# A two-layer decoder trunk with its residual stream held tokens-first: w_out and w_down as 512-column strips past stationary tokens

## The chip, the core and the metric

One core of a Trainium2 chip runs the whole program. The metric is the device time of an execution in microseconds; before the change it is 2322.69 us, the median of three runs (2322.14 to 2322.91). Engines are named as in the profile: PE is TensorE with PEld its weight loads, DVE is VectorE, ACT is ScalarE, POOL is GpSimd, SP is SyncE, which issues the transfers.

## The reference

256 tokens of width 2048 pass through two layers, in float32:

```python
for l in range(DEPTH):
    h = rms_norm(x, attn_norm[l])
    proj = h @ w_in[l]                      # 2048 x 7184, split into heads' q, k, v and gates
    ...                                     # 4 heads of gated linear attention, 4 of retention
    mix = jnp.concatenate([o_gla, o_ret], axis=-1)
    x = x + mix @ w_out[l]                  # 2048 x 2048
    h = rms_norm(x, mlp_norm[l])
    x = x + jnp.square(jax.nn.relu(h @ w_up[l])) @ w_down[l]   # 2048 x 8192, 8192 x 2048
return rms_norm(x, final_norm)              # rms_norm: x * rsqrt(mean(x*x) + eps) * gain
```

## The kernel before

Every product is made of three. A float32 operand is split into a high part (rounded to fp32r by ACT) and a low part (the rest, by DVE), and high·high, high·low and low·high are added up in PSUM. Weights arrive from memory in pieces of 1 MB; each is split in two halves (`split`, one ACT cast `hi` and one DVE subtraction `lo` of 128x1024 each), of which `take` keeps two ahead of PE. The pools hold 3 raw pieces and 4 halves each of `hi` and `lo`, so a half is cast when PE has left the fourth half before it. Activations are tiles `z` of 128 x 512, the high part of 256 tokens beside the low one.

The residual stream `x` lies transposed: 128 features on the partitions, 16 k-tiles, 256 tokens along the free side. Two forms of matmul stand in the program:

- Weights stationary (`mm3`, `mat`; lines 239 and 241): for each k-tile the high weights meet all 512 columns of z and the low weights its 256 high ones. An output tile of 128 features takes 32 matmuls. w_up, w_down, w_out and half of w_in run so. The result of w_out and w_down is added to `x` by two DVE additions of 128x256 (`residual`).
- Tokens stationary (`wide`; lines 477 to 479): each half of the tokens of z is the stationary operand and a strip of up to 512 weight columns passes, three matmuls for each k-tile and token half. The rest of w_in runs so.

A layer is a chain of stages on PE: w_in with the heads between, w_out (16 tiles), then four blocks b, each 16 tiles of w_up (relu squared, split into z) and 16 of w_down. Sums of squares for a norm are made by ACT (`sq`) and DVE (`sqacc`), summed over partitions by matmuls with a column of ones (line 361, `Norm.scale`), made into reciprocal roots on POOL, and `spread` (line 372) turns these by a matmul into a tile R with a token in each column. A norm's gain is applied as x becomes z, R only behind the next product.

The order of the program is that of the code, with a scheduler that moves instructions a little by priority; each engine runs its own in order. `after(n, f)` puts a piece of work n `step()`s later, a step being a tile or a part of a strip.

Of the kernel before, what the change touches and what calls it, by code (L numbers as in the profile page):

```python
# [1 line left out]

# [7 lines left out]
F32 = mybir.dt.float32  # L10
# [6 lines left out]
P = 128  # L17
# [62 lines left out]
KEPT = 7  # L80
# [3 lines left out]
N_ATT, N_MLP, N_FIN, N_GLA, N_INV, N_N = 0, 32, 64, 80, 96, 97  # L84
# [31 lines left out]
def hybrid_kernel(ctx: ExitStack, tc: tile.TileContext, xT, positions, w_first, w_in_t, w_in_w, w_in_v0, w_in_n,  # L116
                  w_out_first, w_out, w_up, w_down, gate_up, norms, rows, consts, out):
# [16 lines left out]
    x = cp.tile([P, KT, S], F32, name="x")  # L134
# [45 lines left out]
    def w_pieces():  # L180
# [6 lines left out]
        for l in range(DEPTH):  # L187
# [67 lines left out]
    def mat_pair(zs):  # L255
# [9 lines left out]
        mm(0, w, range(8, 14))  # L265
        mm(1, take(), range(8))
        mm(0, w, range(14, 16))
# [59 lines left out]
    class Norm:  # L327


        def __init__(self, col):  # L330
            self.col, self.sums, self.z, self.R = col, [], [], None

# [7 lines left out]
        def square(self, k):  # L340
            sq = tmp("sq")
            A.activation(out=sq, in_=x[:, k, :], func=AF.Square)
            if k == 0 or k == KT - 1 and self.col is None:
                self.sums.append(sq)
            else:
                acc = tmp("sqacc")
                tt(acc, self.sums[0], sq, ALU.add)
                self.sums[0] = acc

        def add(self, k):  # L350
            if self.col is not None:
                self.scaled(k)
            self.square(k)

# [510 lines left out]
```

## Time and profile before

| | us |
|---|---|
| median of three runs | 2322.69 |
| the profiled execution | 2323.79 |
| its span, first to last instruction | 2322.0 |
| PE busy | 2297.7 |
| DVE busy | 1604.2 |
| ACT busy | 1059.2 |

PE's matmuls are pipelined: the duration of one holds its way through the array, and one starts before the one ahead of it has ended. Work on PE is therefore read from the distance between starts, or from how many fit into a window.

### The profile page before, as it was taken

What the parts mean: (1) busy time and instruction counts of PE and PEld (TensorE: products, weight loads), DVE (VectorE), ACT (ScalarE), POOL (GpSimd) and SP (SyncE); (2) the same over time, 40 slices, a digit from 0 to 9 for tenths busy, and PEclk for the clock granted to TensorE, in tenths of its full rate; (3) what the DMA queues carried; (4) which work ended last, traced back from release to release, by engine and by line L of the source; (5) the groups of instructions that cost most, each with busy time, mean ns of one, the idle gap of its engine ahead of it and who ended that gap; (6) DMA issues with size and microseconds to landing.
All of it is one profiled execution on the core that took longest, in us unless ns stands there. A gap on an engine that the chain in (4) does not pass through costs nothing.

```text
span 2322.0 us, 32691 instructions
## 1 busy us (share of the span) xinstructions
PE 2297.7 (99%) x13116; PEld 2002.4 (86%) x13116; DVE 1604.2 (69%) x2482; ACT 1059.2 (46%) x1467; POOL 90.6 (4%) x253
## 2 busy tenths in 40 slices
PE   8999999999999999999999999999999999999997
PEld 7888888888888888888898888988888888888886
DVE  7777777676576576577767777776766766766765
ACT  5444544544344344345544444454434434434442
POOL 3001001000000000000000101000000000000000
PEclk9999999999999999999999999999999999999999
DMA  7544545555555555555554445455555555555553
GB/s 258 178 169 177 193 170 183 192 187 184 192 187 189 192 184 197 182 192 189 185 181 179 173 175 178 162 187 184 194 185 189 192 184 196 182 194 187 186 195 109
DMA packets 61034, 429.13 MB, mean 185 GB/s; under 512 B 6849, under 2 KB 7105, under 8 KB 10450
## 3 DMA queue, kind: packets, MB, share of 16 engines
q1 hardware_dynamic: 60738, 427.00, 53.1%
q8 instruction: 102, 1.67, 0.3%
q14 instruction: 50, 0.41, 0.0%
q10 hardware_dynamic: 144, 0.05, 0.0%
HBM read 424.92 MB, written 2.10 MB: 184 GB/s over the span
## 4 chain that ended last, share of the span: by engine, by line
PE 97%; DVE 1%; POOL 1%; issue 0%; DMA 0%; ACT 0%; DVEq 0%; POOLq 0%
PE acc L239 53%; PE acc L241 26%; PE acc L477 5%; PE acc L478 5%; PE acc L479 5%; POOL rs_t L155 1%; PE ps_s L594 0%; PE ps_v L479 0%; PE ps_v L478 0%; PE ps_v L477 0%; PE ps_t L695 0%; PE ps_s L623 0%; DVE z L158 0%; PE ps_o L643 0%; PE ps_o L644 0%
## 5 line engine op out<-in xcount | busy, mean ns | idle before, releaser
L239 PE MATMUL acc<-z,hi 128*128 128x512 f32 x5376 | 1692.8, 396 | 6.7 <-ACT hi L212 6.7
L212 ACT CAST hi<-raw 128x1024 fp32r<-128x1024 f32 (+1 forms) x808 | 840.2, 1042 | 1157.1 <-PE acc L239 752.8
L155 DVE TENSOR_TENSOR lo<-raw,hi 128x1024 fp32r<-128x1024 f32 (+1 forms) x808 | 979.1, 1215 | 516.3 <-ACT hi L212 514.2
L241 PEld LDWEIGHTS acc<-z,lo 128*128 128x128 f32 x5376 | 1011.0, 188 | 242.8 <-DVE lo L155 4.0
L241 PE MATMUL acc<-z,lo 128*128 128x256 f32 x5376 | 1057.9, 278 | 2.4 <-DVE lo L155 2.4
L239 PEld LDWEIGHTS acc<-z,hi 128*128 128x128 f32 x5376 | 820.4, 189 | 9.0 <-ACT hi L212 6.7
L155 DVE TENSOR_TENSOR x<-x,acc 128x256 f32<-128x256 f32 x320 | 133.8, 420 | 126.6 <-PE acc L241 121.7
L477 PE MATMUL acc<-hi,z 128*128 128x512 f32 (+2 forms) x576 | 206.6, 360 | 0.0
L478 PE MATMUL acc<-lo,z 128*128 128x512 f32 (+2 forms) x576 | 204.8, 356 | 0.0
L479 PE MATMUL acc<-hi,z 128*128 128x512 f32 (+2 forms) x576 | 204.6, 355 | 0.0
L479 PEld LDWEIGHTS acc<-hi,z 128*128 128x128 f32 x576 | 109.2, 190 | 15.3
L477 PEld LDWEIGHTS acc<-hi,z 128*128 128x128 f32 x576 | 109.2, 190 | 15.1
L478 PEld LDWEIGHTS acc<-lo,z 128*128 128x128 f32 x576 | 109.3, 190 | 14.3
L155 DVE TENSOR_TENSOR sum<-acc,right 128x256 f32<-128x256 f32 x176 | 73.2, 416 | 3.2 <-ACT right L292 3.2
L292 ACT COPY right<-acc 128x256 f32<-128x256 f32 x176 | 64.4, 366 | 2.2 <-PE acc L241 2.2
L158 DVE SCALAR_TENSOR_TENSOR uu<-ug 128x256 f32<-128x256 f32 x128 | 54.3, 424 | 4.4
L155 DVE TENSOR_TENSOR ug<-sum,R 128x256 f32<-128x256 f32 x128 | 54.4, 425 | 4.2
L540 DVE RECIPROCAL ge<-ge 128x256 f32<-128x256 f32 x32 | 54.6, 1732 | 0.2
L155 DVE TENSOR_TENSOR z<-uu,z 128x256 fp32r<-128x256 f32 x128 | 53.4, 418 | 0.0
L303 ACT CAST z<-uu 128x256 fp32r<-128x256 f32 x128 | 51.5, 404 | 0.1
L155 POOL TENSOR_TENSOR rs_t<-rs_y 128x2 f32<-128x2 f32 x48 | 20.5, 427 | 593.2 <-DVE rs_y L315 590.7
L155 POOL TENSOR_TENSOR rs_t<-r_tok 128x2 f32<-128x2 f32 x12 | 8.8, 731 | 887.1 <-DVE r_tok L315 886.5
(130 smaller groups left out, 757.5 us busy)
## 6 DMA issues: line engine op xcount, KB each, us to landing
raw<-w_up SPq DMA_DIRECT2D x128, 1024.0 KB, 4.9
raw<-w_down SPq DMA_DIRECT2D x128, 1024.0 KB, 4.9
raw<-w_in_w SPq DMA_DIRECT2D x48, 1024.0 KB, 4.8
raw<-w_in_t SPq DMA_DIRECT2D x44, 1024.0 KB, 4.7
raw<-w_out SPq DMA_DIRECT2D x24, 1024.0 KB, 5.0
raw<-w_in_n SPq DMA_DIRECT2D x12, 1024.0 KB, 5.0
raw<-w_out_first SPq DMA_DIRECT2D x8, 1024.0 KB, 5.2
raw<-w_in_v SPq DMA_DIRECT2D x8, 544.0 KB, 4.0
```

Of the source, the lines that this page charges most:

```text
L155: return (e or V).tensor_tensor(out=out, in0=a, in1=b, op=op)
L158: return V.scalar_tensor_tensor(out=out, in0=a, scalar=s, in1=b, op0=op0, op1=op1)
L212: A.copy(out=hi[:, :n], in_=raw)
L239: T.matmul(acc, hi[:, ws[i]], zs[i], start=(k + i == 0), stop=False)
L241: T.matmul(acc[:, :S], lo[:, ws[i]], zs[i][:, :S], start=False, stop=(k + i == KT - 1))
L292: A.copy(out=r, in_=acc[:, S:])
L303: A.copy(out=z[:, :S], in_=src)
L477: T.matmul(ps[t][:, :n], zh, hi[:, ks], start=(k == 0), stop=False)
L478: T.matmul(ps[t][:, :n], zh, lo[:, ks], start=False, stop=False)
L479: T.matmul(ps[t][:, :n], zl, hi[:, ks], start=False, stop=(k == KT - 1))
L540: V.reciprocal(out=e, in_=e)
```

## The change

- x's residual is kept as `xt`, tokens on the partitions, 2 x 2048 numbers each. It's loaded as a second copy of x (`x_tok`, 2 MB) into the place of the transposed x when the first norm has used that.
- w_out and each block of w_down run as four strips of 512 columns past stationary tokens (`strip`), their weights laid out for it in memory. A strip ends in one DVE addition of 128x512 for each half of the tokens.
- Sums of squares come from ACT alone: `Square` over 512 columns with a sum along the row (`TokenNorm.square`), for each strip and token half; DVE adds the four. The matmuls with ones go, but for the first norm.
- For each norm that a product follows, PE transposes `xt` back (`TokenNorm.transpose`): 8 transposes of 128x128 for a strip of 512 features, two steps behind the strip, and those of the last strip between the halves of the first tile of the next product (`mat_pair` with `between`). ACT and DVE make z from the transposes' PSUM. `spread` follows those two tiles.
- The end: the gain is multiplied in as a row (`fin`), the last strip keeps its last four pieces and runs them for one token half and then the other (`kept=4`), and each half is scaled and stored on its own (`finish`), with no matmul.

```diff
-            for i in range(KT // 4):
-                yield w_out_first[l, i], 2
-            for m in range(NFIRST, KT):
-                yield w_out[l, m - NFIRST], 2
+            for c in range(NC):
+                for u in range(4):
+                    yield w_out[l, c, u], 2
             for b in range(NFB):
                 for f in range(FB):
                     yield w_up[l, b * FB + f], 2
-                for m in range(KT):
-                    yield w_down[l, b, m], 2
+                for c in range(NC):
+                    for u in range(4):
+                        yield w_down[l, b, c, u], 2
...
-    def mat_pair(zs):
+    def mat_pair(zs, between):
 
         accs = [new_acc(), new_acc()]
 
@@ -262,29 +264,50 @@
 
         mm(0, take(), range(8))
         w = take()
-        mm(0, w, range(8, 14))
+        between()
+        mm(0, w, range(8, 12))
         mm(1, take(), range(8))
-        mm(0, w, range(14, 16))
+        mm(0, w, range(12, 16))
         mm(1, take(), range(8, 16))
         return accs
 
-    def mats(zs, order, before, done):
+    def strip(zs, order, done, kept=1, every=2):
+
+        ps = [new_acc() for t in range(NT)]
+        left = []
+
+        def mm(u, t, hi, lo):
+            for kk in range(2):
+                z, ks = zs[order[2 * u + kk]], slice(kk * SW, (kk + 1) * SW)
+                zh, zl = z[:, t * P:(t + 1) * P], z[:, S + t * P:S + (t + 1) * P]
+                T.matmul(ps[t], zh, hi[:, ks], start=(u + kk == 0), stop=False)
+                T.matmul(ps[t], zh, lo[:, ks], start=False, stop=False)
+                T.matmul(ps[t], zl, hi[:, ks], start=False, stop=(2 * u + kk == KT - 1))
+
+        for u in range(KT // 2):
+            w = take(AHEAD if u < KT // 2 - kept else min(AHEAD, kept - 1))
+            if u < KT // 2 - kept:
+                for t in range(NT):
+                    mm(u, t, *w)
+                if u % every == every - 1:
+                    step()
+            else:
+                left.append((u, *w))
+        for t in range(NT):
+            for u, hi, lo in left:
+                mm(u, t, hi, lo)
+            done(t, ps[t])
+
+    def mats(zs, before, done):
 
         accs = [new_acc() for _ in range(NFIRST)]
-        kept = []
         for i in range(KT // 2):
             before(i)
             hi, lo = take(min(i, AHEAD))
-            if i < KEPT:
-                for m in range(NFIRST):
-                    mm3(accs[m], hi, lo, (m, NFIRST + m), [zs[order[2 * i + kk]] for kk in range(2)], 2 * i)
-            else:
-                kept.append((hi, lo))
-        for m in range(NFIRST):
-            for i, (hi, lo) in enumerate(kept):
-                k = 2 * (KEPT + i)
-                mm3(accs[m], hi, lo, (m, NFIRST + m), [zs[order[k + kk]] for kk in range(2)], k)
-            done(m, accs[m])
+            for m in range(NFIRST):
+                mm3(accs[m], hi, lo, (m, NFIRST + m), zs[2 * i:2 * i + 2], 2 * i)
+                if i == KT // 2 - 1:
+                    done(m, accs[m])
 
...
-        def square(self, k):
-            sq = tmp("sq")
-            A.activation(out=sq, in_=x[:, k, :], func=AF.Square)
-            if k == 0 or k == KT - 1 and self.col is None:
-                self.sums.append(sq)
-            else:
-                acc = tmp("sqacc")
-                tt(acc, self.sums[0], sq, ALU.add)
-                self.sums[0] = acc
-
-        def add(self, k):
-            if self.col is not None:
-                self.scaled(k)
-            self.square(k)
...
+    class TokenNorm(Norm):
+
+
+        def __init__(self, col):
+            self.col, self.z, self.R = col, [None] * KT, None
+            self.sq = sp.tile([P, NT, NC], F32, tag="sq", name="sq", bufs=2)
+            self.r = cp.tile([P, NT], F32, tag="r_tok", name="r_tok", bufs=2)
+
+        def square(self, c, t, ps):
+            A.activation(out=ps, in_=xt[:, t, c * SW:(c + 1) * SW], func=AF.Square,
+                         accum_out=self.sq[:, t, c:c + 1])
+
+        def transpose(self, c):
+            for k in range(c * SW // P, (c + 1) * SW // P, 2):
+                pt = mxp.tile([P, 2, S], F32, tag="mx", name="ps_x")
+                for i in range(2):
+                    for t in range(NT):
+                        T.transpose(pt[:, i, t * P:(t + 1) * P], xt[:, t, (k + i) * P:(k + i + 1) * P], ident)
+                for i in range(2):
+                    f = self.col + k + i
+                    self.z[k + i] = to_z(pt[:, i, :], nrm[:, f:f + 1])
+
+        def scale(self, e=G, ts=slice(0, NT)):
+            n = ts.stop - ts.start
+            v = sp.tile([P, NT], F32, tag="rv", name="rv")
+            V.tensor_reduce(out=v[:, :n], in_=self.sq[:, ts, :], axis=mybir.AxisListType.X, op=ALU.add)
+            V.tensor_scalar(out=v[:, :n], in0=v[:, :n], scalar1=1.0 / D, scalar2=EPS, op0=ALU.mult, op1=ALU.add)
+            rsqrt(v[:, :n], n, self.r[:, ts], e)
 
     pending, now = [], [0]
 
...
+    def finish(norm, t):
+
+        norm.scale(V, slice(t, t + 1))
+        for i, (a, b) in enumerate(((0, 512), (512, 1024), (1024, 1536), (1536, 2048))):
+            xc = xt[:, t, a:b]
+            if i % 2:
+                A.activation(out=xc, in_=xc, func=AF.Copy, scale=norm.r[:, t:t + 1])
+            else:
+                V.tensor_scalar(out=xc, in0=xc, scalar1=norm.r[:, t:t + 1], scalar2=None, op0=ALU.mult)
+            nc.sync.dma_start(out=out[:, t, a:b], in_=xc)
+
+    mats(norm.z, begin, lambda m, acc: first.append(total(acc)))
     rotary_tables()
 
...
+        def begin_norm():
+            norm.transpose(NC - 1)
+            norm.scale()
+
         plan = w_in_plan()
+        if l:
+            first = [total(a) for a in mat_pair(z_att, begin_norm)]
         for n, (what, g, part, h, _) in enumerate(plan):
             if what == "w":
                 wide(g, n == len(plan) - 1)
             else:
                 d = st.setdefault((g, h), {})
-                a = first[n] if l == 0 and n < NFIRST else total(mat(z_att))
+                a = first[n] if n < len(first) else total(mat(z_att))
                 if part == "k0" and g == "g":
...
@@ -725,30 +776,31 @@
                         first_head = l == 0 and h == 0
                         after(SC + 3 * first_head, ret_scores, h)
                         after(OU + 2 * first_head, head_out, g, h)
-            n0 = NFIRST - 1 if l == 0 else 0
-            if n == n0:
-                norm.scale()
-                after(3 if l == 0 else 2, spread)
+            if n == len(first) - 1:
+                if l == 0:
+                    norm.scale()
+                after(3 if l == 0 else 1, spread)
+            if l == 0 and n == NFIRST + 2:
+                xt = cp.tile([P, NT, D], F32, tag="x", name="xt")
+                nc.sync.dma_start(out=xt, in_=x_tok)
             step()
 
-        def residual(acc, m):
-            tt(x[:, m, :], x[:, m, :], acc[:, :S], ALU.add)
-            tt(x[:, m, :], x[:, m, :], acc[:, S:], ALU.add)
-
-        norm = Norm(N_MLP + l * KT)
-
-        def out_tile(m, acc):
-            residual(acc, m)
-            norm.add(m)
-
-        mats(mix, MIX_ORDER, lambda i: i and step(), out_tile)
-        for m in range(NFIRST, KT):
-            out_tile(m, mat(mix))
+        def add(norm, c, t, ps, fin=None):
+            xc = xt[:, t, c * SW:(c + 1) * SW]
+            tt(xc, xc, ps, ALU.add)
+            if norm is not None:
+                norm.square(c, t, ps)
+                if fin is not None:
+                    tt(xc, xc, fin[:, c * SW:(c + 1) * SW], ALU.mult)
+                elif t == NT - 1 and c < NC - 1:
+                    after(2, norm.transpose, c)
+
+        norm = TokenNorm(N_MLP + l * KT)
+        for c in range(NC):
+            strip(mix, MIX_ORDER, partial(add, norm, c), every=1 if c == 0 else 2)
             step()
 
-        after(1, norm.scale)
-        after(2, norm.spread)
-        nxt = Norm(N_ATT + (l + 1) * KT if l + 1 < DEPTH else None)
+        nxt, fin = None, None
         late = []
 
         def up(a, us, f):
@@ -765,31 +817,29 @@
 
         for b in range(NFB):
             us = [None] * FB
+            if b == 0:
+                two = mat_pair(norm.z, begin_norm)
+                after(1, norm.spread)
             for f in range(FB):
-                a = total(mat(norm.z))
+                a = total(two[f] if b == 0 and f < 2 else mat(norm.z))
                 step()
                 up(a, us, f)
-            accs = mat_pair(us)
-            for m in range(KT):
-                acc = accs[m] if m < 2 else mat(us)
-                residual(acc, m)
-                if b == NFB - 1:
-                    nxt.add(m)
-                    if l + 1 == DEPTH:
-                        V.tensor_scalar(out=x[:, m, :], in0=x[:, m, :], scalar1=nrm[:, N_FIN + m:N_FIN + m + 1],
-                                        scalar2=None, op0=ALU.mult)
+            if b == NFB - 1:
+                nxt = TokenNorm(N_ATT + (l + 1) * KT if l + 1 < DEPTH else None)
+                if l + 1 == DEPTH:
+                    fin = cp.tile([P, D], F32, tag="row", name="fin")
+                    nc.sync.dma_start(out=fin, in_=gain.broadcast_to([P, D]))
+            for c in range(NC):
+                last = fin is not None and c == NC - 1
+
+                def done(t, ps):
+                    add(nxt, c, t, ps, fin)
+                    if last:
+                        finish(nxt, t)
+
+                strip(us, range(KT), done, 4 if last else 1)
                 step()
         norm = nxt
-
-    norm.scale(V)
-    norm.spread(False)
-    R = norm.R.rearrange("p (k s) -> p k s", k=1)
-    k = 0
-    for n in (1, 3, 4, 4, 4):
-        xs = x[:, k:k + n, :]
-        tt(xs, xs, R.broadcast_to([P, n, S]), ALU.mult)
-        nc.sync.dma_start(out=out[:, k:k + n, :], in_=xs)
-        k += n
```

The order on PE within a block of w_down, one output tile and its k-tiles. Before (`z_` are activations, `hi_` and `lo_` one half-piece of weights, `acc_` a bank of PSUM):

```order
L239 MATMUL acc_5873<-z_4736,hi_5831 128x512
L239 MATMUL acc_5873<-z_4790,hi_5831 128x512
L241 MATMUL acc_5873<-z_4736,lo_5832 128x256
L241 MATMUL acc_5873<-z_4790,lo_5832 128x256
L239 MATMUL acc_5873<-z_4844,hi_5831 128x512
L239 MATMUL acc_5873<-z_4898,hi_5831 128x512
```

and now, one piece of a strip (the two banks are the two halves of the tokens):

```order
L283 MATMUL acc_5296<-hi_5388,z_5103 128x512
L284 MATMUL acc_5296<-lo_5389,z_5103 128x512
L285 MATMUL acc_5296<-hi_5388,z_5103 128x512
L283 MATMUL acc_5296<-hi_5388,z_5157 128x512
L284 MATMUL acc_5296<-lo_5389,z_5157 128x512
L285 MATMUL acc_5296<-hi_5388,z_5157 128x512
L283 MATMUL acc_5297<-hi_5388,z_5103 128x512
L284 MATMUL acc_5297<-lo_5389,z_5103 128x512
```

Every matmul now has 512 moving columns, which are weights; a pair of k-tiles takes 12 of them for 512 output columns, where it took 16 of mixed width.

The order on DVE where the first layer's w_out ends and w_up begins. Before (`x_` is the transposed residual, `z_4436` the last k-tile of the MLP's input, `sum` and later rows belong to w_up):

```order
L155 TENSOR_TENSOR lo_4447<-raw_4444,hi_4446 128x1024
L155 TENSOR_TENSOR x_88<-x_88,acc_4391 128x256 x2
L155 TENSOR_TENSOR lo_4467<-raw_4444,hi_4466 128x1024
L158 SCALAR_TENSOR_TENSOR z_4436<-x_88,nrm_90,z_4436 128x256
L155 TENSOR_TENSOR sqacc_4441<-sqacc_4389,sq_4439 128x256
L155 TENSOR_TENSOR lo_4515<-raw_4512,hi_4514 128x1024
L363 TENSOR_SCALAR rv_4493<-ps_r_4490 128x2
```

and now (`acc_4083` and `acc_4084` are the token halves of the last strip, `lo_4256` and `lo_4276` the two halves of w_up's second tile, `ps_x` the transposes):

```order
L157 TENSOR_TENSOR lo_4256<-raw_4253,hi_4255 128x1024
L157 TENSOR_TENSOR xt_787<-xt_787,acc_4083 128x512
L157 TENSOR_TENSOR xt_787<-xt_787,acc_4084 128x512
L157 TENSOR_TENSOR lo_4276<-raw_4253,hi_4275 128x1024
L411 TENSOR_REDUCE rv_4301<-sq_3545 128x2
...
L157 TENSOR_TENSOR lo_4330<-raw_4327,hi_4329 128x1024
L160 SCALAR_TENSOR_TENSOR z_4284<-ps_x_4279,nrm_90,z_4284 128x256
```

The last four z of the next product stand behind the two additions, a reduction and two casts of later weights; before, the last z stood behind two additions and one cast. On PE the same place reads, before:

```order
L239 MATMUL acc<-z,hi 128x512 x2
L241 MATMUL acc<-z,lo 128x256 x2
L361 MATMUL ps_r<-cst,sqacc 128x1 x2
L239 MATMUL acc<-z,hi 128x512 x2
L241 MATMUL acc<-z,lo 128x256 x2
```

and now, from the strip's last matmuls to the second half of w_up's first tile:

```order
L284 MATMUL acc<-lo,z 128x512
L285 MATMUL acc<-hi,z 128x512
L241 MATMUL acc<-z,hi 128x512 x2
L243 MATMUL acc<-z,lo 128x256 x2
...
L243 MATMUL acc<-z,lo 128x256 x2
L403 MATMUL ps_x<-cst,xt 128x128 x8
L241 MATMUL acc<-z,hi 128x512 x2
```

Between the strip and the eight transposes stand 16 matmuls, the first eight k-tiles of one tile of w_up.

## Rows read from the trace of the kernel before

**Rows 1.** The page: PE's busy time, and the chain that ended last, by engine.
```profile
PE 2297.7 (99%) x13116; PEld 2002.4 (86%) x13116; DVE 1604.2 (69%) x2482; ACT 1059.2 (46%) x1467; POOL 90.6 (4%) x253
...
PE 97%; DVE 1%; POOL 1%; issue 0%; DMA 0%; ACT 0%; DVEq 0%; POOLq 0%
```

**Rows 2.** Windows (from:to, length; busy and count by engine; PEclk, DMA share, GB/s).
```profile
549.00:638.00 89.00, 89.00 (x513) 77.68 (x512) 53.29 (x67) 34.17 (x34) 0.00 (x0) 1.00 0.58 195
```

**Rows 3.** Timeline of PE (start, length, count) in a tile of w_down.
```profile
599.96 0.63 PE L239 MATMUL acc<-z,hi 128*128 128x512 f32 x2
600.42 0.39 PE L241 MATMUL acc<-z,lo 128*128 128x256 f32 x2
600.65 0.63 PE L239 MATMUL acc<-z,hi 128*128 128x512 f32 x2
```

**Rows 4.** Timeline of PE, a w_in strip: its first matmul, and what follows its 48th.
```profile
138.36 0.40 PE L477 MATMUL acc<-hi,z 128*128 128x512 f32 x1
...
149.28 0.60 PE L695 MATMUL ps_t<-cst,on 128*128 128x128 f32 x4
```

**Rows 5.** Timeline of PE, a head's four transposes and what follows them.
```profile
371.38 0.60 PE L695 MATMUL ps_t<-cst,on 128*128 128x128 f32 x4
371.74 0.72 PE L239 MATMUL acc<-z,hi 128*128 128x512 f32 x2
372.30 0.40 PE L241 MATMUL acc<-z,lo 128*128 128x256 f32 x2
```

**Rows 6.** Timeline of PE behind w_out: the sums of squares, and spread.
```profile
452.88 0.50 PE L361 MATMUL ps_r<-cst,sqacc 128*128 128x1 f32 x4
453.24 0.70 PE L239 MATMUL acc<-z,hi 128*128 128x512 f32 x2
...
459.36 0.71 PE L372 MATMUL ps_R<-cst,r_tok 128*128 128x128 f32 x4 [0.30 <-POOL r_tok L155]
```

**Rows 7.** Lines (names, shapes, count | busy us, mean ns of one | idle before).
```profile
L155 DVE TENSOR_TENSOR lo<-raw,hi 128x1024 fp32r<-128x1024 f32 (+1 forms) x808 | 979.1, 1215 | 516.3 <-ACT hi L212 514.2
...
L212 ACT CAST hi<-raw 128x1024 fp32r<-128x1024 f32 (+1 forms) x808 | 840.2, 1042 | 1157.1 <-PE acc L239 752.8 <-issue 209.8 <-PE acc L479 135.3
...
L155 DVE TENSOR_TENSOR x<-x,acc 128x256 f32<-128x256 f32 x320 | 133.8, 420 | 126.6 <-PE acc L241 121.7
...
L306 ACT ACTIVATE z<-ps_t,nrm 128x256 fp32r<-128x256 f32 x16 | 7.6, 474 | 14.3 <-DVE z L158 14.3
...
L427 ACT ACTIVATE z<-x 128x512 f32<-128x512 f32 x8 | 4.9, 616 | 0.0
```

**Rows 8.** Timeline of the end of the program.
```profile
2306.99 0.39 PE L241 MATMUL acc<-z,lo 128*128 128x256 f32 x2
2307.42 0.88 DVE L155 TENSOR_TENSOR x<-x,acc 128x256 f32<-128x256 f32 x2 [3.52 <-PE acc L241]
...
2309.66 0.16 DVE L363 TENSOR_SCALAR rv<-ps_r 128x2 f32<-128x2 f32 x1 [0.53 <-PE ps_r L361]
...
2311.82 0.16 DVE L158 SCALAR_TENSOR_TENSOR r_tok<-rs_t,r_tok 128x2 f32<-128x2 f32 x1
...
2313.30 4.68 DVE L155 TENSOR_TENSOR x<-x,ps_R 128x256 f32<-128x256 f32 x5 [1.31 <-PE ps_R L372]
```

**Rows 9.** DMA issues of the output (count, KB each, median us to landing).
```profile
y<-x SPq DMA_DIRECT2D x3, 512.0 KB, 2.9
...
y<-x SPq DMA_DIRECT2D x1, 384.0 KB, 2.4
```

**Rows 10.** Timeline of SP in the first w_in: three loads of one strip.
```profile
24.64 7.66 SPq L223 DMA_DIRECT2D raw<-w_in_v  x3
```

**Rows 11.** Timeline of PE: the first use of the w_in_n pieces.
```profile
50.37 0.59 PE L477 MATMUL acc<-hi,z 128*128 128x256 f32 x2
```

**Rows 12.** Timeline of PE: the spread of the first norm.
```profile
41.76 1.06 PE L372 MATMUL ps_R<-cst,r_tok 128*128 128x128 f32 x4 [1.81 <-POOL r_tok L155]
```

**Rows 13.** Window of PE behind that spread (columns as rows 2, PE alone).
```profile
42.50:45.20 2.70, 2.70 (x14) 0.50 0.19 79
```

More of the change, by code (lines that the diff above doesn't have):

```diff
@@ L1 @@
 from contextlib import ExitStack
+from functools import partial
 import numpy as np
@@ L79 @@
 AHEAD = 2
-KEPT = 7
+NC = 4
+SW = D // NC
 X_CUTS = {0: (2, 4), 1: (4, 6), 2: (6, 10), 4: (10, 16)}
@@ L116, in hybrid_kernel @@
 def hybrid_kernel(ctx: ExitStack, tc: tile.TileContext, xT, positions, w_first, w_in_t, w_in_w, w_in_v0, w_in_n,
-                  w_out_first, w_out, w_up, w_down, gate_up, norms, rows, consts, out):
+                  w_out, w_up, w_down, gate_up, norms, rows, gain, x_tok, consts, out):
     nc = tc.nc
@@ L132, in hybrid_kernel @@
     V, A, G, T = nc.vector, nc.scalar, nc.gpsimd, nc.tensor
-    x = cp.tile([P, KT, S], F32, name="x")
+    x = cp.tile([P, KT, S], F32, tag="x", name="x")
     cst = cp.tile([P, C_N], F32, name="cst")
@@ L330, in __init__ @@
         def __init__(self, col):
-            self.col, self.sums, self.z, self.R = col, [], [], None
+            self.col, self.z, self.R = col, [], None
         def scaled(self, k):
@@ L366, in scale, with spread @@
             self.r = r
-        def spread(self, keep=True):
+        def spread(self):
             ps = mxp.tile([P, 512], F32, tag="mx", name="ps_R")
@@ L373, in spread @@
                          start=True, stop=True)
-            if keep:
-                R = cp.tile([P, S], F32, tag="R", name="R", bufs=2)
-                A.copy(out=R, in_=ps[:, :S])
-                self.R = R
-            else:
-                self.R = ps[:, :S]
+            R = cp.tile([P, S], F32, tag="R", name="R", bufs=2)
+            A.copy(out=R, in_=ps[:, :S])
+            self.R = R
+    class TokenNorm(Norm):
[21 more added lines that the diff above has]
+            rsqrt(v[:, :n], n, self.r[:, ts], e)
     pending, now = [], [0]
@@ L406, in load_x @@
         nc.sync.dma_start(out=x[:, a:b, :], in_=xT[:, a:b, :])
-    norm = Norm(N_ATT)
+    norm, xt = Norm(N_ATT), None
     sqs = ztile().bitcast(F32)
-    norm.sums = [sqs]
+    norm.sums = sqs
     first = []
@@ L431, in begin @@
             rotary_angles()
-    mats(norm.z, range(KT), begin, lambda m, acc: first.append(total(acc)))
+    def finish(norm, t):
[8 more added lines that the diff above has]
+    mats(norm.z, begin, lambda m, acc: first.append(total(acc)))
     rotary_tables()
@@ L833 @@
     wides = [np.concatenate([w_in[:, :, p[3]:p[3] + p[4]] for p in parts], axis=2) for parts, _ in wide_plan()]
-    w_out_first = a["w_out"].reshape(DEPTH, KT, P, D)[:, MIX_ORDER, :, :NFIRST * P]
+    chunks = lambda w: np.stack(np.split(w, NC, axis=-1), axis=-3)
+    w_out = a["w_out"].reshape(DEPTH, KT, P, D)[:, MIX_ORDER].reshape(DEPTH, D, D)
     w_down = a["w_down"].reshape(DEPTH, NFB, FB * P, D)
+    x = a["x"][0]
     arrays = {
-        "xT": np.ascontiguousarray(a["x"][0].reshape(S, KT, P).transpose(2, 1, 0)),
+        "xT": np.ascontiguousarray(x.reshape(S, KT, P).transpose(2, 1, 0)),
         "positions": np.ascontiguousarray(a["positions"]),
@@ L843 @@
         "w_in_n": strips_of(np.stack([w for w in wides if w.shape[2] == DV], axis=1), 2),
-        "w_out_first": first_of(w_out_first.reshape(DEPTH, D, NFIRST * P), 4),
-        "w_out": tiles_of(a["w_out"][:, :, NFIRST * P:]),
+        "w_out": strips_of(chunks(w_out), 4),
         "w_up": tiles_of(a["w_up"]),
-        "w_down": tiles_of(w_down),
+        "w_down": strips_of(chunks(w_down), 4),
         "gate_up": np.ascontiguousarray(
@@ L850 @@
         "norms": np.ascontiguousarray(np.concatenate(
-            [columns(a[n]) for n in ("attn_norm", "mlp_norm", "final_norm", "gla_out_norm")]
+            [columns(a[n]) for n in ("attn_norm", "mlp_norm", "gla_out_norm")]
             + [(10000.0 ** (-np.arange(0, DV, 2) / DV)).astype(np.float32)[:, None]], axis=1)),
         "rows": np.ascontiguousarray(np.concatenate([a["ret_norm_gain"], a["ret_norm_bias"]], axis=1)),
+        "gain": a["final_norm"][None],
+        "x_tok": np.ascontiguousarray(x.reshape(NT, P, D).transpose(1, 0, 2)),
         "consts": constants(),
@@ L858 @@
             for n, v in arrays.items()]
-    args.append(nc.dram_tensor("y", (P, KT, S), F32, kind="ExternalOutput").ap())
+    args.append(nc.dram_tensor("y", (P, NT, D), F32, kind="ExternalOutput").ap())
     with tile.TileContext(nc) as tc:
@@ L863 @@
     y = r.results[0]["y"]
-    return np.ascontiguousarray(y.transpose(2, 1, 0)).reshape(1, S, D)
+    return np.ascontiguousarray(y.transpose(1, 0, 2)).reshape(1, S, D)
```

4 lines of the change are left out of this document (2 added, 2 removed).

## The prediction

> **What bounds the kernel now.** I read the busy time of each engine first, then the chain of waits, then TensorE (PE) in order of time in four places. PE is busy for 2297.7 of 2322.0 us, and the chain that ended last is 97% PE [rows 1]. So a change counts by what it does to the spacing of matmuls on PE, and at the two ends of the program, where PE isn't fed. The stretches by window say that a stage of 16 tiles is stall-free: some 512 matmuls in 89.0 us at granted clock 1.00, the 2.4 GHz level, with VectorE busy for 53.3 us and ScalarE for 34.2 [rows 2]. The timeline of one such tile shows the beat: two matmuls of 256 columns take 0.23 us together [rows 3], and of the mean beat of four, 89.0 / 128 = 0.695 us, 0.465 are left for the two of 512 columns. That is 116 and 232.5 ns a matmul, start to start; the durations printed in those rows overlap and are no spacing.
>
> The strips that the change brings to w_out and w_down have a model in the kernel of before: the 512-column strips of w_in, where tokens are stationary. There 48 matmuls of 512 columns run from 138.36 to 149.28 us, 227.5 ns each [rows 4].
>
> **Term 1, the strips.** A stage (w_out, or one block of w_down) multiplies 16 k-tiles by 16 column tiles. Before: 256 matmuls of 512 columns and 256 of 256, 196,608 columns, 89.0 us [rows 2]. After: 16 k-tiles x 4 strips x 2 token halves x 3 products = 384 matmuls of 512 columns, the same 196,608 columns in 128 instructions fewer. At 227.5 ns that is 87.4 us, 1.6 us less. There are 2 x (1 + 4) = 10 such stages: -16.4 us. No row shows such a strip in these stages, so the bounds are the two spacings of a 512-column matmul in this trace: 227.5 ns [rows 4] gives -16.4, 232.5 ns [rows 2, 3] gives 10 x (384 x 0.2325 - 89.0) = +2.8. I take the lower, since that row is the same instruction sequence (zh·hi, zh·lo, zl·hi, all 512 wide) and 232.5 belongs to a 512 that alternates with 256s. A gain beyond -16.4 would need a spacing that no row has; I allow 1 ns either side, some 4 us.
>
> **Term 2, the transposes.** Three norms (both MLP norms and the second layer's first) now get their input by 32 transposes each, in 12 groups of 8. Four transposes of a head take from 371.38 to 371.74, and the pair of 512s behind them 0.56 us instead of 0.465 [rows 5]. Eight: twice 0.36 plus some 0.07, since only the last of a group overlaps its successor, plus 0.09, so 0.88 us. 12 x 0.88 = +10.6 us, bounds 9.7 (twice 0.36 + 0.09) and 11.6 (0.97 with the pairs wholly apart).
>
> **Term 3, the sums of squares by matmul.** For those three norms the group of four L361 goes: 452.88 to 453.24 [rows 6], and the same 0.09 us behind it, 0.45 us. -1.3 us.
>
> **Term 4, the wait of spread.** PE sits 0.30 us for POOL's r_tok before the spread, which stands one tile (5.6 us) behind the sums [rows 6]. Now the spread stands behind two tiles and the sums need no PE. 3 x 0.3 = -0.9 us, between 0 and -0.9.
>
> **Term 5, the end.** Before: the last matmuls end at about 2307.22 (2306.99 plus 0.23), the add starts at 2307.42, the reciprocal root runs from 2309.66 to 2311.98, then come the spread and five products with their stores; the products end at 2317.98, and 4.0 us for the last issue, its landing (2.9 us of 512 KB) and the closing follow, to 2322.0 [rows 3, 8, 9]. That is 14.8 us behind the last matmul. After: token half 0 is finished beneath the last 24 matmuls of half 1 (24 x 0.2275 = 5.5 us). For half 1: 0.2 to start; an add of 128x512, 0.70 (between 0.42 for 256 and 1.215 for 1024 elements); a square of 128x512, 0.62; gaps 0.1; reduction 0.2 and the same root 2.3; two scalings on ScalarE 1.3; the same 4.0 less 0.7, since a 256 KB store should land in 2.2 us (384 KB took 2.4); 0.5 for the queue of four issues [rows 7 to 9]. Sum 9.2 us. -5.6 us; with add and square at either neighbour's price (0.42 to 1.2 each) -6.1 to -4.5.
>
> **What costs nothing, and its cover.** At each of the three hand-overs the last transposes need the add of the second token half. Let T be the end of a strip. The order rows put one low-part cast and both adds on VectorE ahead. That cast needs the buffer which PE frees at T - 2.7 (12 matmuls earlier): rounding 1.04, cast 1.2, so it ends near T - 0.3; adds end near T + 0.4 and T + 1.1 [rows 7]. PE runs 16 matmuls, four beats of 0.70 us, first: the transposes start at T + 2.8. Cover 1.7 us. Their z are wanted at T + 2.8 + 0.9 + 4.2 = T + 7.9 at the earliest; behind one more rounding, four scalings of 0.47 and their low parts are done at about T + 7.2, and the last two of them are wanted at T + 8.6. The residual adds fall from 32 x 0.42 to 8 x 0.70 us a stage on VectorE, off the path. At the other strip borders three pieces are cast ahead of the adds and the fourth, behind them, is wanted 8.2 us after T (36 matmuls of the next strip), so no price. If the cover goes, see rival C.
>
> The token copy of x (2.1 MB) is issued on SP when the third of a strip's w_in_v loads is out, at 32.30, ahead of the two w_in_n loads, whose strip starts at 50.37 [rows 10, 11]. At the 195 GB/s of rows 2 the copy lasts until 43.1, one w_in_n load behind it until 48.5; rounding and low part (1.04 + 1.2) end at 50.7, the high part at 49.5. Cost 0 to 0.5 us; I take 0. The 1 MB for the final gain goes out where layer 1 has its row load.
>
> **Sum.** -16.4 + 10.6 - 1.3 - 0.9 - 5.6 = -13.6 us. The profiled execution took 2323.8 (its span 2322.0 and 1.8 around it): 2310.2 after. The median of the runs shown, 2322.69, is 1.1 below it: 2309.1, so 2309 us.
>
> **Rivals.** A: matmuls cost by column, not by instruction. Then 196,608 columns cost 89.0 us whatever their cut, term 1 is 0 and the sum +2.8: 2325.5 us, which is no change. For it: the columns make most of a stage, and a quarter fewer instructions change the spacing by under 2% in the rows there are. Against it: 1536 columns take 695 ns in four matmuls [rows 2] and 3 x 227.5 = 682.5 ns in three [rows 4], so the fourth instruction costs 12.5 ns.
> The Trainium skill, "TensorE: Matmul & The Clock Gate", section "Back-to-back issue gap", puts that fixed part at about 2.5 ns: by it the 128 instructions are worth 0.32 us a stage, term 1 an estimated -3.2 us, and the sum about zero. The trace doesn't agree (12.5 ns), so A gets little.
>
> B, the slower one: in w_out and w_down a 512-column matmul keeps the 232.5 ns that it has there now, because these stages carry more transfers and casts (DMA share 0.58 [rows 2]) than the w_in strip of rows 4. Place: all 10 stages; price +2.8 instead of -16.4, so +5.6 in all: 2328.3 us, and 3.8 us more for each further ns. It decides from 10 x (384 s - 89.0) + 2.8 > 4.6, a spacing s above 232.2 ns. Against it: rows 3 mix two widths, rows 4 don't, and both run beside casts of the same kind of pieces.
>
> C: the cover at the hand-overs fails (casts late, VectorE's queue in another order). PE then waits as ahead of 41.76, 1.8 us, behind which the granted clock was 0.50, the 1.2 GHz level, for 2.7 us [rows 12, 13], of which half is lost: 3.2 us at each of three places, +9.5: 2318.6 us.
>
> **Chances.** Forecast 0.78, A 0.09, B 0.07, C 0.06. About 0.2%, 4.6 us, is what a measurement here can tell from no change. Forecast and half of C are faster (0.80, a hundredth taken off for a forecast that runs short), A, the rest of C and that hundredth are no change (0.12), B and a hundredth of A are slower (0.08). Forecast with its own bounds (strip spacing 1 ns either way 4, transposes 1, end 1, small waits up to 5 more): 2303 to 2317; with C to 2320. A and B lie outside.
>
> **What would show it.** PE's matmul records fall from 13116 by 1280 + 20 + 4 and rise by 96, to about 11,908. A w_down stage takes 87.4 us with matmuls 227 ns apart; 232 or more says B, 89.0 A. Each group of eight transposes delays PE by 0.9 us. No idle PE longer than 0.3 us from 50 us on, and clock 1.00 throughout; a wait on VectorE before the transposes, or on a z in the second tile behind a strip, says C. The span ends 9 to 10 us behind the last matmul. The forecast is wrong if the spacing of the strips isn't that of rows 4.

## The result, and the profile after

The changed kernel takes 2308.44 us (median of 4 runs, 2307.11 to 2309.43), beside 2322.44 for the kernel before in 4 runs: ratio 0.9939, 95% interval [0.9922, 0.9956]. A second set of runs gave 2308.25 against 2323.14, 0.9936 [0.9924, 0.9949]. The forecast was 2309.0. The profiled execution took 2307.11 us with a span of 2305.3, 16.7 us shorter than the span of before; the medians are 14.0 apart, so one profiled execution of each flatters the change by about 2.7 us.

The page after, in answer to [rows 1]:

```profile
PE 2281.8 (99%) x11908; PEld 1949.2 (85%) x11908; DVE 1507.1 (65%) x2191; ACT 1057.6 (46%) x1471; POOL 88.1 (4%) x253
...
PE 98%; DVE 1%; DMA 0%; issue 0%; ACT 0%; POOL 0%; ACTq 0%; DVEq 0%
```

PE is still the bound, with the 11,908 matmuls that were forecast. Next, windows cut exactly from a stage's first matmul to the next stage's first (from:to, length, busy and count by engine, granted clock, DMA share, GB/s): of before one block of w_down,

```profile
716.30:805.47 89.17, 89.17 (x514) 77.80 (x513) 52.62 (x66) 34.10 (x35) 0.00 (x0) 1.00 0.56 190
```

and of after the same block of w_down, a block of w_up, and the first w_up behind a norm:

```profile
716.08:803.13 87.05, 87.05 (x386) 72.08 (x385) 44.51 (x43) 34.30 (x34) 0.00 (x0) 1.00 0.55 192
626.92:716.08 89.16, 89.16 (x513) 77.80 (x512) 62.99 (x94) 42.27 (x62) 0.00 (x0) 1.00 0.54 191
449.38:539.87 90.49, 90.49 (x526) 79.14 (x524) 65.25 (x102) 45.58 (x71) 3.36 (x12) 1.00 0.54 188
```

A block of w_down falls by 2.12 us, at the same clock of 1.00 (the 2.4 GHz level) and with PE busy throughout in both. A block of w_up, whose code is the same, stays at 89.17 (before, 627.13 to 716.30) and 89.16. w_out, which holds three groups of transposes as well, goes from 91.60 to 92.09.

The hand-over from w_out to w_up in the timeline of after, where a strip ends at T = 449.38 (start, length, engine, operation, count, idle before):

```profile
449.09 1.28 DVE L157 TENSOR_TENSOR xt<-xt,acc 128x512 f32<-128x512 f32 x2
...
449.15 0.39 PE L285 MATMUL acc<-hi,z 128*128 128x512 f32 x1
449.38 0.62 PE L241 MATMUL acc<-z,hi 128*128 128x512 f32 x2
...
451.93 0.39 PE L243 MATMUL acc<-z,lo 128*128 128x256 f32 x2
452.16 1.04 PE L403 MATMUL ps_x<-cst,xt 128*128 128x128 f32 x8
452.95 0.70 PE L241 MATMUL acc<-z,hi 128*128 128x512 f32 x2
...
461.16 0.40 PE L243 MATMUL acc<-z,lo 128*128 128x256 f32 x2
461.39 0.61 PE L380 MATMUL ps_R<-cst,r_tok 128*128 128x128 f32 x4
461.75 0.71 PE L241 MATMUL acc<-z,hi 128*128 128x512 f32 x2
```

Both additions are done at 450.37, the transposes start at 452.16, and eight of them hold the next matmul up to 452.95. The spread waits for nothing, where it waited 0.30 us before [rows 6]. Around that spread, the timeline of before has

```profile
458.66 0.40 PE L241 MATMUL acc<-z,lo 128*128 128x256 f32 x2
...
459.83 0.71 PE L239 MATMUL acc<-z,hi 128*128 128x512 f32 x2
```

so that the way from the 256s ahead of it to the 512s behind it falls from 1.17 us to 0.59.

The end of after, in answer to [rows 8]:

```profile
2294.66 0.39 PE L285 MATMUL acc<-hi,z 128*128 128x512 f32 x1
2295.09 0.69 DVE L157 TENSOR_TENSOR xt<-xt,acc 128x512 f32<-128x512 f32 x1
2295.81 0.60 ACT L395 ACTIVATE acc<-xt 128x512 f32<-128x512 f32 x1 [0.23 <-DVE xt L157]
2296.34 0.19 ACT L395 ACTIVATION_READ_ACCUMULATOR acc<-xt 128x1 f32 x1
2296.56 0.69 DVE L157 TENSOR_TENSOR xt<-xt,fin 128x512 f32<-128x512 f32 x1 [0.79 <-ACT acc L395]
2297.17 0.15 DVE L411 TENSOR_REDUCE rv<-sq 128x1 f32<-128x4 f32 x1
...
2299.66 1.33 ACT L473 ACTIVATE xt<-xt,r_tok 128x512 f32<-128x512 f32 x2 [3.13 <-DVE r_tok L160]
```

The last matmul starts at 2294.66 and the span ends at 2305.3.

One thing got worse. PE's waits up to 75 us (engine, tile and line, what it waited for, us in total, times, longest) are, before,

```profile
PE acc L239 <- ACT hi L212: 6.7, 1, 6.7
PE acc L241 <- DVE lo L155: 2.4, 2, 2.2
PE ps_R L372 <- POOL r_tok L155: 1.8, 1, 1.8
```

and after:

```profile
PE acc L241 <- ACT hi L214: 7.2, 1, 7.2
PE acc L243 <- DVE lo L157: 3.0, 2, 2.3
PE ps_R L380 <- POOL r_tok L157: 1.8, 1, 1.8
PE ps_gr L552 <- ACT gr L535: 0.5, 1, 0.5
PE ps_o L687 <- DMA raw<-w_in_t: 0.5, 1, 0.5
PE acc L523 <- DVE lo L157: 0.2, 1, 0.2
```

The last three are new. They sit between 49 and 56 us. ScalarE's timeline there shows why; before:

```profile
48.58 1.05 ACT L212 CAST hi<-raw 128x1024 fp32r<-128x1024 f32 x1 [0.85 <-PE acc L479]
...
53.44 0.84 ACT L498 ACTIVATE vh<-acc,r_tok 128x256 fp32r<-128x256 f32 x2
```

and after:

```profile
46.17 0.65 ACT L214 CAST hi<-raw 128x544 fp32r<-128x544 f32 x1 [0.85 <-PE acc L524]
53.03 0.84 ACT L543 ACTIVATE vh<-acc,r_tok 128x256 fp32r<-128x256 f32 x2 [6.21 <-PE acc L524]
...
54.98 0.51 ACT L435 CAST s_hi<-s 128x384 fp32r<-128x384 f32 x1 [0.26 <-DVE s L157]
55.39 1.04 ACT L214 CAST hi<-raw 128x1024 fp32r<-128x1024 f32 x1
```

ScalarE idles 6.21 us with `vh` at the head of its queue, and the casts of w_in_n, which stood ahead of it, now stand behind. The wait of ps_o is put down to a load, but its matmul reads `s_hi`, whose cast ends at 55.49; PE starts at 55.54.

### The profile page after: what moved, and what is told of

It is laid out like the page before. It is cut to its first block, busy times and chain, and to the rows that moved or that the text cites. A ratio compares the mean times of both kernels' runs of the same rounds, so it can differ in the third digit from the quotient of the medians.

```text
span 2305.3 us, 30023 instructions
## 1 busy us (share of the span) xinstructions
PE 2281.8 (99%) x11908; PEld 1949.2 (85%) x11908; DVE 1507.1 (65%) x2191; ACT 1057.6 (46%) x1471; POOL 88.1 (4%) x253
## 4 chain that ended last, share of the span: by engine, by line
PE 98%; DVE 1%; DMA 0%; issue 0%; ACT 0%; POOL 0%; ACTq 0%; DVEq 0%
PE acc L241 28%; PE acc L243 14%; PE acc L285 13%; PE acc L284 13%; PE acc L283 13%; PE acc L522 5%; PE acc L523 5%; PE acc L524 5%; PE ps_s L639 0%; PE ps_x L403 0%; PE ps_v L524 0%; PE ps_v L523 0%; PE ps_v L522 0%; DVE lo L157 0%; PE ps_t L740 0%; PE ps_o L688 0%
## 5 line engine op out<-in xcount | busy, mean ns | idle before, releaser
L241 PE MATMUL acc<-z,hi 128*128 128x512 f32 x2816 | 887.9, 397 | 7.2 <-ACT hi L214 7.2
L243 PEld LDWEIGHTS acc<-z,lo 128*128 128x128 f32 x2816 | 529.8, 188 | 129.4 <-DVE lo L157 4.6
L243 PE MATMUL acc<-z,lo 128*128 128x256 f32 x2816 | 554.6, 278 | 3.0 <-DVE lo L157 3.0
L283 PE MATMUL acc<-hi,z 128*128 128x512 f32 x1280 | 499.2, 390 | 0.0
L285 PE MATMUL acc<-hi,z 128*128 128x512 f32 x1280 | 498.1, 389 | 0.0
L284 PE MATMUL acc<-lo,z 128*128 128x512 f32 x1280 | 498.1, 389 | 0.0
L241 PEld LDWEIGHTS acc<-z,hi 128*128 128x128 f32 x2816 | 431.3, 189 | 9.2 <-ACT hi L214 7.2
L285 PEld LDWEIGHTS acc<-hi,z 128*128 128x128 f32 x1280 | 240.3, 188 | 49.9
L284 PEld LDWEIGHTS acc<-lo,z 128*128 128x128 f32 x1280 | 240.3, 188 | 49.2
L283 PEld LDWEIGHTS acc<-hi,z 128*128 128x128 f32 x1280 | 240.3, 188 | 49.1
L523 PEld LDWEIGHTS acc<-lo,z 128*128 128x128 f32 x576 | 108.7, 189 | 15.6 <-DVE bs L693 0.8
L522 PEld LDWEIGHTS acc<-hi,z 128*128 128x128 f32 x576 | 108.5, 189 | 15.7 <-ACT hi L214 0.8
L524 PEld LDWEIGHTS acc<-hi,z 128*128 128x128 f32 x576 | 108.7, 189 | 15.2
```

The costliest lines, as they stand in the source:

```text
L241: T.matmul(acc, hi[:, ws[i]], zs[i], start=(k + i == 0), stop=False)
L243: T.matmul(acc[:, :S], lo[:, ws[i]], zs[i][:, :S], start=False, stop=(k + i == KT - 1))
L283: T.matmul(ps[t], zh, hi[:, ks], start=(u + kk == 0), stop=False)
L284: T.matmul(ps[t], zh, lo[:, ks], start=False, stop=False)
L285: T.matmul(ps[t], zl, hi[:, ks], start=False, stop=(2 * u + kk == KT - 1))
L522: T.matmul(ps[t][:, :n], zh, hi[:, ks], start=(k == 0), stop=False)
```

## The experiments

s256, twice_t, alt, no_cover and kept1 ran once each. The runs of one kernel lie up to 2.4 us apart (2307.22 to 2309.61 for the changed one), so these five are read by their stages. From w_out on, those repeat within 0.02 us between two profiles of the changed kernel.

**The strips' matmuls in two.** Is the gain of a strip a price per instruction? In the kernel s256 the matmuls of a strip, all but the first and last for each token half, are cut into two of 256 columns: 94 instructions for 48, 368 more in a stage.

```diff
-                T.matmul(ps[t], zh, hi[:, ks], start=(u + kk == 0), stop=False)
...
+                    n = SW if a or b else SW // 2
+                    for q in range(0, SW, n):
+                        T.matmul(ps[t][:, q:q + n], w, m[:, kk * SW + q:kk * SW + q + n], start=a, stop=b)
```

> The changed kernel with nearly every strip matmul (46 of 48 of a strip and token half) issued as two of 256 columns: the same columns, 368 instructions more in each of the 10 stages. Theory (a matmul costs 13 ns beside its columns): 736 of 256 columns at the 120 ns that such matmuls take in w_in, and 16 of 512 at 226.7, make 91.9 us of a stage of 87.05, 49 us in all, so about 2357 us. Rival (cost goes by columns, and the strips gained by what is stationary or by there being no narrow matmul with a weight load it can't hide, not by their number): a stage stays within 1 us of 87.05. By the 2.5 ns a matmul that the Trainium skill, TensorE: Matmul & The Clock Gate, section Back-to-back issue gap, gives, an estimated 0.9 us a stage more.

It took 2355.25 us. The window of its block of w_down:

```profile
725.16:817.12 91.96, 91.96 (x754) 91.26 (x753) 44.81 (x43) 34.14 (x34) 0.00 (x0) 1.00 0.52 183
```

91.96 less 87.05 is 4.91 us for 368 instructions on the same columns, 13.3 ns each. That is also what is left of 87.05 / 384 = 226.7 ns if 512 columns go at 2.4 GHz, one a cycle (213.3, an estimate that the trace of s256 bears out: its 256s start 119.9 ns apart, so 256 columns more take 107). Rival A falls for good. By the 2.5 ns that the Trainium skill, "TensorE: Matmul & The Clock Gate", section "Back-to-back issue gap", gives for an isolated matmul, it would have been an estimated 0.92 us. This trace, where every matmul brings its own weight load, doesn't agree; the figure beside rival A was the same one, set against a stream.

What the 13.3 ns consist of stays open. Each of the 368 came with a load of its own (PEld x753), and in s256 the loads fill 91.26 of 91.96 us, so no run here tells the price of a matmul from that of its load.

**Every transpose twice.** Does a transpose delay PE by its whole spacing?

```diff
-                for i in range(2):
+                for i in (0, 1, 0, 1):
```

> The changed kernel with every group of eight transposes issued twice into the same PSUM (96 transposes more). Theory (transposes stand on PE's path in full): each of the 12 groups delays PE by 0.8 to 0.9 us more, w_out 2.6 us longer, the first w_up of each layer 0.9, the whole about 10 us longer than the changed kernel (near 2318.5 us). Rival (they hide under waits that PE has anyway, and the 10 us of the prediction were made up by something else): under 3 us longer.

It took 2317.03 us, 8.6 above the median of the changed kernel; the spans are 9.8 apart, 10.5 more in the stages with transposes and 0.7 less ahead of w_out. The first w_up behind a norm, with one group of eight more:

```profile
451.33:542.69 91.36, 91.36 (x533) 80.01 (x532) 65.21 (x102) 45.66 (x71) 3.36 (x12) 1.00 0.53 186
```

91.36 less 90.49 is 0.87 us for eight. w_out, which holds three groups, grew by 2.61 (94.70 after 92.09). The spacing within a group is 0.109 us, so all of it lies on the path and nothing of it hides. The first copy of a group costs the same: w_out less 3 x 0.87 is 89.48, 2.12 below before, just what a block of w_down gains.

**The transposes ahead of w_up.** Does the cover of 16 matmuls at the hand-over earn its place? `between()` moves ahead of the tile's first matmuls.

```diff
+        between()
         mm(0, take(), range(8))
         w = take()
-        between()
```

> The changed kernel with the last strip's transposes put ahead of the first matmuls of the next product instead of behind eight k-tiles. Theory (the cover was needed: the second half's residual add ends about 1.1 us behind the strip): PE waits 0.5 to 1 us at each of three places, with a short stretch at the lower clock at most, so 2 to 5 us longer in all. Rival (the cover was idle, the add is done in time anyway): within 0.5 us.

It took 2307.21 us, no slower. The timeline of the hand-over:

```profile
448.92 1.28 DVE L157 TENSOR_TENSOR xt<-xt,acc 128x512 f32<-128x512 f32 x2
...
449.65 0.20 PEld L403 LDWEIGHTS ps_x<-cst,xt 128*128 128x128 f32 x2 [0.25 <-DVE xt L157]
449.67 0.43 PE L403 MATMUL ps_x<-cst,xt 128*128 128x128 f32 x2
...
450.41 0.82 PE L403 MATMUL ps_x<-cst,xt 128*128 128x128 f32 x6
```

and the window of the stage:

```profile
449.21:539.77 90.56, 90.56 (x526) 79.05 (x524) 65.03 (x102) 45.34 (x71) 3.17 (x12) 1.00 0.54 188
```

The scheduler put two matmuls of w_up ahead of the first two transposes and more between these and the other six, so the experiment took away most of the cover, not all. The stage grew by 0.07 us. What it shows: most of the 1.8 us of cover (additions done at T + 1.0, transposes at T + 2.8) was idle here, and rival C wasn't near. What a hand-over with no cover at all costs wasn't tried.

**The order of widths.** The gain of a block of w_down is 2.12 us, and 128 instructions of 13.3 ns explain 1.71. Are the other 0.41 the price of mixing 512s with 256s? In the kernel alt the weights-stationary tiles run one 512 and one 256 in turn, for two and two.

```diff
         for i in range(2):
             T.matmul(acc, hi[:, ws[i]], zs[i], start=(k + i == 0), stop=False)
-        for i in range(2):
             T.matmul(acc[:, :S], lo[:, ws[i]], zs[i][:, :S], start=False, stop=(k + i == KT - 1))
```

> The changed kernel with the weights-stationary tiles (w_up, most of w_in) issued as high, low, high, low instead of high, high, low, low. The same matmuls in the same number. Theory (a fixed cost for each instruction): w_up stays at 89.17 us a stage. Rival (the mixed stages lose because two 256-column matmuls in a row can't hide a weight load, and the strips win because no narrow one is left): a stage of w_up changes by over 0.5 us, downwards if alternation hides the load.

It took 2317.69 us. I had expected no change. A block of w_up:

```profile
627.22:717.66 90.44, 90.44 (x514) 78.39 (x512) 62.98 (x94) 42.20 (x62) 0.00 (x0) 1.00 0.53 188
```

1.28 us more for the same instructions: order alone has a price. It is upwards, where the expectation's rival had the stage fall if alternation hid a weight load. Does the price fall with fewer changes of width? The kernel group8 (built on the faster kernel best, below) runs eight 512s and then eight 256s:

```diff
-            for kk in range(0, 8, 2):
-                mm3(acc, hi, lo, (kk, kk + 1), zs[8 * u + kk:8 * u + kk + 2], 8 * u + kk)
+            mm3(acc, hi, lo, range(8), zs[8 * u:8 * u + 8], 8 * u)
...
```

> The kernel 'best' (x_late with the last product in another tile), where the weights-stationary tiles run eight matmuls of 512 columns with the high weights and then eight of 256 with the low ones, in place of two and two. Theory: a matmul that follows one of another width costs more. The alternating order had 256 changes of width more in a stage of w_up and took 1.28 us more, 5 ns a change; groups of eight have 192 changes fewer, so a w_up stage falls from 89.2 to between 88.2 (5 ns a change) and 88.85 (the 0.41 us of 256 changes that the strips' gain leaves over, 1.6 ns a change), and the whole, 8 such stages and about 3 more stages' worth in w_in, by 3 to 10 us against 'best': 2294 to 2301 us. Rival: only the direct alternation costs (two of a width next to each other hide it), a stage stays at 89.2 and the time at 2304.

```profile
624.21:713.57 89.36, 89.36 (x514) 78.66 (x512) 63.00 (x94) 42.93 (x63) 0.00 (x0) 1.00 0.55 194
```

Three rows of its timeline, eight wide, eight narrow and the next eight wide:

```profile
643.73 2.00 PE L241 MATMUL acc<-z,hi 128*128 128x512 f32 x8
645.58 1.11 PE L243 MATMUL acc<-z,lo 128*128 128x256 f32 x8
646.53 2.00 PE L241 MATMUL acc<-z,hi 128*128 128x512 f32 x8
```

The stage grew by 0.20 us, and the whole took 2306.99 against 2303.92 of best beside it. So a price per change of width, which I had read out of alt, is wrong. In the trace the 512s that follow eight 256s start 233, 236, 228, 232 and 231 ns apart and only then 227, while the first 256 takes 113 instead of 120. A change back to wide costs for some five matmuls there; behind a pair of 256s, where w_up gives way to a strip in after, only the first two are slow (232 and 231). At 226.7 and 120 ns throughout, the 512 matmuls of a w_up stage would take an estimated 88.75 us: twos pay 0.41 for mixing, eights 0.61, alternation 1.69. So the 0.41 that the strips gain beyond their number is the price of the mix, and twos are the best of the three orders that ran. What makes it so stays open.

**Keeping the load of the token copy in its place.** The load `x_tok` goes out at 32.98 in after. In the kernel x_late it is bound to the program's order, six tiles later:

```diff
-            if l == 0 and n == NFIRST + 2:
+            if l == 0 and n == NFIRST + 8:
                 xt = cp.tile([P, NT, D], F32, tag="x", name="xt")
-                nc.sync.dma_start(out=xt, in_=x_tok)
+                tc.keep_in_program_order(nc.sync.dma_start(out=xt, in_=x_tok))
```

> The changed kernel with the token copy of x issued later, behind three of the w_in_t loads, so that ACT again casts the w_in_n pieces ahead of vh, as in the kernel before. Theory (the 1.6 us of waits on PE between 49 and 56 us come from that order of casts): these waits go, the first w_in takes about 1.5 us less, the whole 1 to 1.6 us less than the changed kernel. Rival (they come from the 2 MB themselves): the waits move to where the copy now is, and nothing is gained.

The changed kernel ran beside it once more:

> The changed kernel once more, for the interval: 0.994 of the kernel before, 14 us less.

x_late took 2304.63 us (0.9922 [0.9908, 0.9935]) where the changed kernel took 2308.25. PE's waits up to 75 us are now:

```profile
PE acc L241 <- ACT hi L214: 6.9, 1, 6.9
PE acc L243 <- DVE lo L157: 2.9, 2, 2.1
PE ps_R L380 <- POOL r_tok L157: 1.8, 1, 1.8
```

The three new waits, 1.2 us, are gone, and ScalarE's first cast of w_in_n is back ahead of `vh`, at 46.85. The edit both moves the load and binds it, so which of the two restored the order isn't told apart. The first w_in takes 347.19 us instead of 350.07. Part of these 2.9 us is the clock at the start, which was granted at 1.00 between 20 and 28 us in this profile and at 0.79 in that of after. The kernel best, below, has the late load too, and 0.79 there: its first w_in takes 347.73. So at the same clock the late load is worth 2.3 us, 1.2 of them the three waits; the rest I can't divide. Against the kernel before, the early load cost only 1.0 us in sum, beside a clock that was granted at 0.76 from 42 to 49 us before and at 1.00 after. That clock, which the prediction didn't have, gave back an estimated 7.00 x 0.24 = 1.7 us; best, at 0.79 earlier on and without the early load, is 1.3 us below the kernel before in this stage.

**The end: keeping four pieces or one.** Does running one token half ahead of the other pay?

```diff
-                strip(us, range(KT), done, 4 if last else 1)
+                strip(us, range(KT), done, 1)
```

> The changed kernel with kept=1 in the last strip too: the first token half ends 6 matmuls ahead of the second instead of 24. Theory (the finish of the first half, some 5.3 us on DVE and ACT, is hidden beneath 24 matmuls): the end grows by about 4 us, 5.45 less 1.36, if DVE works off one half behind the other, by 1 to 2 us if the halves interleave. Rival (the end is set by the stores): no longer.

2309.1 us in one run. The last stage with the end takes 99.86 us instead of 97.47, 2.39 more, between the 1 to 2 us expected of halves that interleave and the 4 of halves one behind the other. The two roots on VectorE run partly interleaved:

```profile
2297.62 0.28 DVE L157 TENSOR_TENSOR rs_t<-r_tok 128x1 f32<-128x1 f32 x2
```

**The best version.** best is x_late, with the last product by the gain written to another tile, so that it needn't wait for the square that reads the same columns.

```diff
-                    tt(xc, xc, fin[:, c * SW:(c + 1) * SW], ALU.mult)
+                    o = xc
+                    if c == NC - 1:
+                        o = norm.tail = rawp.tile([P, 2 * WP], F32, tag="raw", name="raw")[:, :SW]
+                    tt(o, xc, fin[:, c * SW:(c + 1) * SW], ALU.mult)
...
```

> x_late, and the last strip's product with the final gain written to another tile, so that it needn't wait for the square that reads the same columns. Theory (the product stood 0.8 us behind the square on the path of the end): 0.6 us less at the end, with x_late about 2 us less than the changed kernel. Rival (DVE is the same engine for both and the sum of squares sets the end): no more than x_late gives.

```profile
2292.71 0.69 DVE L157 TENSOR_TENSOR xt<-xt,acc 128x512 f32<-128x512 f32 x1 [0.57 <-PE acc L285]
...
2293.43 0.60 ACT L395 ACTIVATE acc<-xt 128x512 f32<-128x512 f32 x1 [0.84 <-DVE xt L157]
2293.43 0.69 DVE L157 TENSOR_TENSOR raw<-xt,fin 128x512 f32<-128x512 f32 x1
...
2294.19 0.16 DVE L411 TENSOR_REDUCE rv<-sq 128x1 f32<-128x4 f32 x1
```

Square and product now start together, and the last stage with the end is 96.89 us, 0.59 less. best took 2304.09 us (0.9918 [0.9904, 0.9931]), and once more beside group8:

> The kernel 'best' once more, beside 'group8' on the same chip: 2304 us, w_up stages of 89.2 us.

2303.92 us, 0.9921 [0.9907, 0.9934]. It beats the kernel before and the changed one (2307.22 to 2309.61 beside it, best at most 2304.43); against x_late alone the 0.5 us of its medians is too little for these intervals, and it rests on the stage.

## Why the prediction was right, and where it was off

The forecast of 2309.0 held, by the mechanism it named. Stage by stage, between the two profiles, with the 0.87 us of twice_t for a group of transposes:

| term | forecast, us | measured, us | from |
|---|---|---|---|
| 1 strips | -16.4 | -21.2 | 10 x (87.05 - 89.17) |
| 2 transposes | +10.6 | +10.4 | 12 x 0.87 |
| 3, 4 sums and spread | -2.2 | -3.1 | 3 x (90.49 - 0.87 - 90.65) |
| 5 end | -5.6 | -4.4 | last stage 97.47 for 103.96, less the strips' 2.12 |
| start and first w_in | 0 to +0.5 | +1.6 | first matmul at 7.22 for 6.66; 350.07 for 349.05 |
| sum | -13.6 | -16.7 | spans 2322.0 and 2305.3 |

- **Term 1** was right in kind and 4.8 us short, beyond the 4 us allowed. Two readings failed. The window of [rows 2] counted 513 matmuls in 89.00 us, but those cut by its borders count as whole ones, and the true stage is 89.17, worth 1.7 us in ten stages. The 227.5 ns of [rows 4] divided a stretch with its edges by 48: in the trace of before that strip's first five matmuls, behind 256s, are spaced 233, 236, 228, 233 and 231 ns, its last 232, and those between 226.7, as the strips of after are; that is 3.1 us.
- **Rivals A and B** fell: the stage wasn't 89.0 us, and the spacing did not stay at 232.5 ns, though the strips ran at a DMA share of 0.55. The reason given against B, that rows 3 mix two widths, holds in its direction: a mixed order can cost more. The simple form, a price per change, does not.
- **Term 2** was right to 0.01 us a group.
- **Terms 3 and 4** were 0.3 us a place short, all of it in term 4. The late r_tok cost 1.17 - 0.59 = 0.58 us, not the 0.30 that [rows 6] print as idle: that is counted from the modelled end of the matmul ahead to the late start, and neither the overlap of the two nor the slow start behind the wait is in it. With the 0.45 of term 3 it makes the 1.03 us measured.
- **The cover** came as worked out: additions done at T + 1.0 (forecast T + 1.1), transposes at T + 2.8. Rival C did not show; PE waits nowhere between 75 and 2285 us. Nor does the price that C put on a wait hold each time: in after PE waits the same 1.8 us ahead of the first norm's spread, and the clock is granted at 1.00 from 40 to 49 us.
- **Term 5** was 1.2 us too good, just outside its own bounds. The working counted the add, the square and the root, and left out that the product by the gain writes the columns which the square reads: it waits 0.79 us behind the add, then takes its own 0.69, and 0.19 goes to reading the accumulator. So the reduction starts at 2297.17, 0.66 later than the working has it (2296.51); best wins back 0.59 of that. The other 0.5 lies behind the last scaling: from its end at 2300.99 to the end of the span are 4.3 us, for which the working had 3.8.
- **The token copy** was priced at 0 to 0.5 us by its transfer. At least 1.2 of its 2.3 us came in another way: with the load there, ScalarE's queue had another order, and the casts got behind instructions that waited 6.21 us. The rest stays open. "No idle PE above 0.3 us from 50 us on" was wrong at two places of 0.5 us.

That the time came out near 2309 owes something to errors of both signs: the gain in terms 1 to 4 was 5.9 us larger than forecast, the two ends 2.8 us worse. The 3.1 us that remain are in the spans; the medians show 0.7 of them, since the profiled execution of after lies 1.3 us below its median and that of before 1.1 above.

## What to carry to other kernels

Where PE is busy throughout, count its instructions as well as its columns: here each matmul with the load of its weights cost 13.3 ns beyond its columns, so fewer and wider ones, all of one width, pay. Measure a stage from its first matmul to the next stage's first, since a window's count includes the matmuls that its borders cut. A load put early into a program with a scheduler is priced by looking at every queue's order around it, not by its bytes alone.

## What the hardware showed that was not expected

- The same 512 matmuls take 89.16, 89.36 or 90.44 us by their order alone (two and two, eight and eight, in turn), at a granted clock of 1.00.
- Behind eight 256-column matmuls five 512s in a row are spaced 228 to 236 ns instead of 226.7 (group8), behind a pair two, at 232 and 231 (after).
- Transposes of 128 columns start 109 ns apart, hardly closer than the 120 ns of the 256-column matmuls among their like in group8.
- The clock between 20 and 28 us was granted at 0.79 to 0.81 in some profiles and at 1.00 in others, also between kernels whose code is the same up to the first w_out: 0.79 in after and no_cover, 1.00 in twice_t and s256. From 42 to 49 us, behind the same wait of 1.8 us, it was 0.76 in before and 1.00 in every profile of the changed kernel and its variants. Nothing here settles why.
- An idle time printed beside a late matmul is less than what the wait costs: 0.30 us printed, 0.58 lost.
